# Last quarter of a feed-forward down product as five and two block products, with the second token half's norm and gate first

## The chip, the core and the metric

The kernel runs on one core of one Trainium2 chip. The metric is the device time of one launch in microseconds (us). The kernel before took 765.87 us (median of 3 runs, 765.47 to 766.1).

## The reference

One inference step of one encoder layer, for 512 prompt tokens and 64 sample tokens, 1024 features, float32. The part that matters here:

```python
x = layer_norm(ALPHA * x + mix @ w_o, ln1_g, ln1_b)
hid = square(relu(x @ w_up))                             # 1024 -> 4096
x = layer_norm(ALPHA * x + hid @ w_down, ln2_g, ln2_b)   # 4096 -> 1024
gate = sigmoid(x @ w_ple_gate + b_ple_gate)              # 1024 -> 1024
y = x + gate * (pe @ w_ple)
```

All 576 tokens go through it together; in the kernel features lie on the partitions and tokens along the free dimension. The attention ahead of it is the same in both kernels.

## The kernel before, in words

**Products.** Every operand is split into a high part (a cast to the rounded 32-bit matmul type) and a low part (the operand minus the high part), and each product is three matmuls per 128-row slice: high weight by high operand, high by low, low by high. `gemm` (L288) issues them and gives control back after every 6; that is one *tick*. `drive` counts ticks, runs the evacuations that were put off with `later(delay, ...)`, and lets a background generator (a layer norm) take steps in proportion.

**The feed-forward in quarters.** The 4096 hidden features come in eight groups of 512 (g = 0..7), two groups to a quarter (q = 0..3). For each quarter, `up_pair` makes the hidden features and `down_pair` adds their share of `w_down` to Y. From the second quarter on, and for the down products of the first three, a 2x2 block product (two 512-row halves of the contraction, two 128-column halves of the outputs, two 288-token halves A and B) is done by `seven` with seven block products in place of eight. A block product is 4 slices x 3 = 12 matmuls of 288 columns, two ticks; they come in the order 11, t0, t1, 21, t3, t2, 22. For them the operand has seven forms: three of its four quarters as they are and four sums (`operands`, L1339 to L1385: rows "11", "12", "22", "s1" to "s4"), each with a cast on ACT (L1351) and a subtraction on DVE (L1349), the sums on DVE too (L1364, L1372, L1374, L1379). The seven sums of the weights are made from three loads of 512, 512 and 256 KB, the first of them with a second, accumulating load on top (L210, from POOL's queue), and two DVE additions (L181, L184).

**The last quarter before.** Its hidden features are made by `seven` as well, but its down product is done plainly by `down_last`: the operand is only cast and subtracted (L1356, L1357), 8 weight units of 512 KB are loaded, and 192 matmuls follow for tokens 0 to 255 (A2), then 192 for tokens 256 to 575 (B2), each evacuated by L1631 on DVE.

**Norm and gate.** `LayerNorm` is a generator with hand-set waits: sums of Y over features (POOL at L1152 and L1154, the last sum and the fold at L1154 and L1159 on DVE), a mean by matmul (L1180), four subtractions (L1184), squares on ACT (L1186, L1189) and their sums (L1190), a variance by matmul (L1200), a square root and a reciprocal (L1202, L1203), a spread to all partitions by PE transposes (L56), and for each of four pairs of feature slices scale (DVE, L1216), gain and bias (ACT, L1227), cast (ACT, L1229) and subtraction (DVE, L1233). L2A (tokens A2) runs beside `down_last` of B2, L2B (tokens B2) beside the gate product of A2. `gate` and `gate_one` do 192 matmuls per token part, then a sigmoid (ACT, L1706, L1724), two DVE operations (L1709, L1710) and the store. PL, the per-layer embedding's product, is read back from DRAM (L1681, 2304 KB) after `seven`.

**What sets the order.** `Weights` is a planner: it loads weights ahead on SP's queue (L208) into four raw tiles of 512 KB (and one small one), and splits them piece by piece, one piece a tick, with a cast on ACT (L149) and a subtraction on DVE (L155; on POOL for units added with `pool_l`), into a ring of five tiles (`whl`). A unit may be split only when it is less than five units ahead of the oldest one in use, `lag` ticks after that one changed; an accumulated load counts as landed 13 ticks after its issue. Five more ring tiles (pool `fe`) come when the tiles of `seven` are given up. A scheduler then orders each engine's instructions, in which `high_priority` brings instructions forward; each engine runs its own list in order.

Of the kernel before, what the change touches and what calls it, by code (L numbers as in the profile page):

```python
# [14 lines left out]
D = 1024  # L15
# [21 lines left out]
def tile_hybrid_step(ctx: ExitStack, tc: tile.TileContext, I, O):  # L37
# [79 lines left out]
    class Weights:  # L117
# [74 lines left out]

        def load(self, issue=True, force=False):
# [176 lines left out]
    G_DOWN = 6  # L370
# [748 lines left out]
    A2, B2 = slice(0, 256), slice(256, NT)  # L1119
# [14 lines left out]
    class LayerNorm:  # L1134


        def __init__(self, sl, gi, waits):
# [3 lines left out]
            self.ready = -1  # L1141
            self.gen = self.steps()
            self.s = None

        def add(self, j):
# [3 lines left out]
            if j == 0:  # L1149
                self.s = lnp[0].tile([128, 2, 320], F32, name="ln_s", tag="ln_s" if self.sl.start else "relu", bufs=1 if self.sl.start else 2)[:, :, :self.w]  # L1150
            elif j == 2:
                (DVE if self.sl is A else POOL).tensor_tensor(self.s, y[:, 0:2], y[:, 2:4], OP.add)  # L1152
            else:
                (DVE if j == 6 or self.sl is A else POOL).tensor_tensor(self.s, self.s, y[:, j:j + 2], OP.add)  # L1154
# [17 lines left out]
        def steps(self):  # L1172
            sl, gi, w = self.sl, self.gi, self.w
            y = Y[:, :, sl]
# [8 lines left out]
            for j in range(0, 8, 2):  # L1183
                DVE.tensor_tensor(y[:, j:j + 2], y[:, j:j + 2], mb, OP.subtract)  # L1184
                if j == 0:
                    ACT.activation(ss, y[:, 0:2], AF.Square)  # L1186
                else:
                    sq = lnp[0].tile([128, 2, 320], F32, name="ln_sq", bufs=2)[:, :, :w]
                    ACT.activation(sq, y[:, j:j + 2], AF.Square)  # L1189
                    DVE.tensor_tensor(ss, ss, sq, OP.add)  # L1190
                if j == 6:
                    self.fold(ss)
# [18 lines left out]

            first = tc.high_priority if sl.start == 0 else ExitStack
# [95 lines left out]
    hid = {}  # L1308
# [5 lines left out]
    def sets(g):  # L1314

        if g >= G_DOWN:
            hid[g] = base.tile([128, 2, 4, NT], F32R, name="hidE", tag="AL") if g % 2 == 0 else \
                fb.tile([128, 2, 4, NT], F32R, name="hidO", tag="hidO")
            return
# [20 lines left out]
    def operands(g, m, t, v):  # L1340
# [12 lines left out]

        if g >= G_DOWN:
# [3 lines left out]
            return  # L1358
# [26 lines left out]
    def up_half(g, c, m, sl):  # L1385
        t = (A, B).index(sl)
        r = lnp[0].tile([128, 2, 320], F32, name="relu", bufs=2)[:, :, :HW]
# [149 lines left out]
    def up_pair(g, m):  # L1537
# [7 lines left out]
        def target(t):  # L1545
            return HX["f"][:, t, b] if g < G_DOWN and g % 2 == 0 else P.r[:, t]
# [62 lines left out]
    def down_last(sl, ln):  # L1609

        w = sl.stop - sl.start
        g0 = NG - 2
        ms = {}
        n = 0
        todo = [(j, 0) for j in (0, 2, 4)] + [(0, 1), (2, 1), (6, 0), (4, 1), (6, 1)]
        for j, part in todo:
            if part == 0:
                ms[j] = psum_g()
            m = ms[j]
            g = g0 + part  # L1620
# [212 lines left out]
```

## Time and profile before

| | us |
|---|---|
| median of 3 runs | 765.87 |
| the profiled execution's own time | 765.81 |
| its span | 764.1 |
| PE busy in the span | 751.4 |
| DVE busy | 571.4 |
| ACT busy | 472.6 |
| POOL busy | 110.6 |

The profile is one execution on the chip. PE's busy time includes the overlap of pipelined matmuls, so 98% busy does not say that PE runs at its peak; waits of PE are read from the list of waits and the chain. Durations of neighbouring DVE or ACT instructions overlap a little as well, so a merged row such as "3.02 x4" tells what four in a row cost. Line numbers (L288) are those of the kernel before. The span of 764.1 us and the 1.7 us around it make the execution's 765.81 us.

### The profile page before, as it was taken

How to read it: one execution, taken by the hardware profiler on the slowest of the kernel's cores; microseconds unless marked ns; L12 is line 12 of the kernel's file. 1: busy time of each engine (PE TensorE's matmuls, PEld its weight loads, DVE VectorE, ACT ScalarE, POOL GpSimd, SP SyncE). 2: the span in 40 equal slices, each digit the busy share in tenths (PEclk: the TensorE clock that was granted, in tenths of full speed). 3: DMA queues.
4: the chain of work that ended last, by engine and by line, in shares of the span. 5: the costliest groups of instructions: out<-in, count | busy, mean ns of one | idle time of the engine just before them, and what ended most of it. 6: DMA issues, size and time to landing. Idle time of an engine off the chain costs nothing.

```text
span 764.1 us, 14624 instructions
## 1 busy us (share of the span) xinstructions
PE 751.4 (98%) x5679; PEld 730.8 (96%) x5679; DVE 571.4 (75%) x1119; ACT 472.6 (62%) x931; POOL 110.6 (14%) x130
## 2 busy tenths in 40 slices
PE   9999999999999999999999999999999999999997
PEld 7999988999899999999999999999999999999997
DVE  6788888888777866779777579866898766657643
ACT  6589777897676535797654577435764466525451
POOL 7100324344241000100000000000000000011000
PEclk9999999999999999999999999999999999999999
DMA  8538354245222325352447666667667664731001
GB/s 284 171 69 152 125 141 121 91 138 173 88 86 81 110 64 174 116 171 86 111 111 178 148 158 175 147 161 184 157 143 181 152 151 152 286 113 30 28 29 69
DMA packets 38197, 101.35 MB, mean 133 GB/s; under 512 B 6000, under 2 KB 10224, under 8 KB 38000
## 3 DMA queue, kind: packets, MB, share of 16 engines
q1 hardware_dynamic: 34384, 87.61, 37.5%
q0 software_dynamic: 3456, 12.58, 10.2%
q8 instruction: 44, 0.72, 0.4%
q10 hardware_dynamic: 288, 0.22, 0.1%
q14 instruction: 25, 0.20, 0.1%
HBM read 85.26 MB, written 9.54 MB: 124 GB/s over the span
## 4 chain that ended last, share of the span: by engine, by line
PE 77%; DVE 13%; ACT 8%; issue 2%; DVEq 0%; ACTq 0%
PE g L288 40%; PE m L288 14%; PE n L288 13%; PE T L56 2%; DVE dbias L693 2%; ACT xr L771 2%; DVE whl L155 2%; DVE m L691 1%; PE V L958 1%; ACT whl L149 1%; PE m L452 1%; DVE sP L891 1%; PE m L466 1%; DVE x L774 1%; PE S L883 1%
## 5 line engine op out<-in xcount | busy, mean ns | idle before, releaser
L149 ACT CAST whl<-wraw 128x1024 fp32r<-128x1024 f32 (+2 forms) x190 | 154.9, 828 | 80.9 <-PE g L288 46.3
L155 DVE TENSOR_TENSOR whl<-wraw,whl 128x1024 fp32r<-128x1024 f32 (+2 forms) x158 | 157.7, 1008 | 53.3 <-ACT whl L149 52.6
L288 PE MATMUL m<-AH,whl 128*128 128x288 f32 x736 | 176.7, 307 | 0.0
L288 PE MATMUL g<-BH,whl 128*128 128x288 f32 (+2 forms) x768 | 160.0, 298 | 0.0
L288 PEld LDWEIGHTS m<-AH,whl 128*128 128x128 f32 x736 | 126.4, 188 | 1.7 <-issue 1.0
L288 PEld LDWEIGHTS g<-BH,whl 128*128 128x128 f32 x768 | 125.0, 188 | 1.5 <-ACT BH L1229 0.2
L288 PE MATMUL g<-BL,whl 128*128 128x288 f32 (+2 forms) x384 | 113.6, 296 | 0.6 <-DVE BL L1233 0.6
L288 PE MATMUL m<-AL,whl 128*128 128x288 f32 x368 | 108.8, 296 | 0.0
L288 PEld LDWEIGHTS g<-BL,whl 128*128 128x128 f32 x384 | 72.3, 188 | 1.2 <-DVE BL L1233 1.1
L288 PEld LDWEIGHTS m<-AL,whl 128*128 128x128 f32 x368 | 69.5, 189 | 0.7
L210 POOL DMA_DIRECT2D wraw<-in_w_dram x24 | 20.7, 864 | 287.5 <-DMA wraw<-in_w_dram 184.8
L896 ACT ACTIVATE sP<-sP,st 128x128 f32<-128x128 f32 (+4 forms) x72 | 39.4, 549 | 35.1 <-DVE st L891 35.0
L155 POOL TENSOR_TENSOR whl<-wraw,whl 128x512 fp32r<-128x512 f32 x32 | 42.2, 1333 | 89.2 <-ACT whl L149 85.0
L288 PE MATMUL m<-BH,whl 128*128 128x288 f32 x192 | 42.9, 302 | 0.0
L288 PE MATMUL g<-s,whl 128*128 128x288 f32 x288 | 42.1, 295 | 0.0
L288 PE MATMUL n<-BH,whl 128*128 128x288 f32 x192 | 42.0, 294 | 0.0
L288 PEld LDWEIGHTS g<-s,whl 128*128 128x128 f32 x288 | 39.5, 188 | 0.0
L56 PE MATMUL T<-ident,sP 128*128 128x128 f32 (+1 forms) x176 | 31.3, 274 | 1.5 <-DVE sP L905 0.6
L288 PEld LDWEIGHTS m<-BH,whl 128*128 128x128 f32 x192 | 32.0, 188 | 0.5 <-issue 0.3
L288 PEld LDWEIGHTS n<-BH,whl 128*128 128x128 f32 x192 | 32.0, 188 | 0.0
L1505 ACT ACTIVATE g<-n 128x288 f32<-128x288 f32 x24 | 9.5, 395 | 35.6 <-PE n L288 35.6
L288 PE MATMUL m<-BL,whl 128*128 128x288 f32 x96 | 28.3, 295 | 0.0
(327 smaller groups left out, 1624.1 us busy)
## 6 DMA issues: line engine op xcount, KB each, us to landing
wraw<-in_w_dram SPq DMA_DIRECT2D x48, 512.0 KB, 3.8
wraw<-in_w_dram POOLq DMA_DIRECT2D x24, 512.0 KB, 5.8
wraw<-in_w_qkv_dram SPq DMA_DIRECT2D x23, 512.0 KB, 3.6
wraw<-in_w_dram SPq DMA_DIRECT2D x24, 256.0 KB, 4.3
wraw<-in_w_up_dram SPq DMA_DIRECT2D x8, 512.0 KB, 4.1
wraw<-in_w_down_dram SPq DMA_DIRECT2D x8, 512.0 KB, 4.2
wraw<-in_w_gate_dram SPq DMA_DIRECT2D x8, 512.0 KB, 4.5
wraw<-in_w_o_dram SPq DMA_DIRECT2D x8, 384.0 KB, 3.0
```

Source lines behind the costliest of these rows:

```text
L56: PE.transpose(out, in_, ident[:n, :n])
L149: ACT.copy(self.hv[u][:, 0, c], src["tile"][:, c])
L155: eng.tensor_tensor(t[:, 1, c], src["tile"][:, c], f(t[:, 0, c]), OP.subtract)
L210: POOL.dma_start(t[:, :n], it["acc"], accum_op=OP.add)
L288: mm = PE.matmul(ps, W(w, kw, wc), a[:, ka, cols], start=(first and i == 0), stop=(last and i == n - 1), skip_group_check=more)
L452: PE.matmul(mk[:, h, :HW], w0(part, k), a[:, k, h * HW:(h + 1) * HW], start=(k == 0 and i == 0), stop=(k == 7 and i == 2))
L466: PE.matmul(acc[b][:n[b], :304], a[:, k, b * 128:b * 128 + n[b]], ixw(part, k), start=(k == 0 and i == 0), stop=(k == 7 and i == 2))
L691: tc.keep_in_program_order(DVE.max(m, s))
L693: tc.keep_in_program_order(DVE.match_replace(out=s, in_to_replace=m, in_values=s, imm_value=GONE))
L771: q(lambda r=r, s=s: ACT.mul(v2(xr[r * 32:r * 32 + 32]), v[s * 32:s * 32 + 32], sc))
L896: ACT.activation(j["P"], j["P"], AF.Exp, bias=j["st"][:, 0:1], scale=-1.0, accum_out=j["st"][:, 2:3])
L1505: ACT.mul(P.e, P.o, -1.0)
```

## The change

The last quarter's down product becomes 4 x 5 block products over all output pairs (`five`: 11, t0, t1, t3, t2) and then 4 x 2 (`two`: the rows "12" and "s4" with plain weight units of 256 output columns). The five finish the B half (tokens 288 to 575) of an output pair; the two complete the A half. The last two groups get the seven operand forms that the others have (L1356 and L1357 go), with the forms of `two` put off by 6 ticks. The weights for `five` are four units with one plain, one accumulated and one more plain load each (three of the four ring tiles that a unit of `seven` takes; one of them half filled and subtracted on POOL); those for `two` are four units of 512 KB subtracted on POOL, where there were eight subtracted on DVE. PL's load is issued before `five`. The norm of B (L2B, waits 5, 9, 3, its instructions at high priority, its work tiles carved out of two tiles of the feed-forward) runs beside `two`, the gate of B follows with the norm of A beside it, then the gate of A. Both token parts are 288 wide, where they were 256 and 320. The five extra ring tiles come after `two`, where they came ahead of `down_last`.

```diff
+        def add_five(self, ap):
+            u = len(self.cs)
+            self.cs += [128] * 3
+            r1 = self.source(ap[:, 0:1024], acc=ap[:, 1024:2048])
+            r2 = self.source(ap[:, 2048:3072])
...
+            self.split(u, r2, [lo], POOL)
+            self.split(u + 1, r1, [all2], DVE)
+            self.piece(u + 1, None, t1, r1, r2)
+            self.piece(u + 2, None, t2, r2)
+            self.split(u + 2, r2, [all2], DVE)
...
-        for kind, n in (("P", 4 if q else 0), ("Q", 4 if q < 3 else 0)):
+        for kind, n in (("P", 4 if q else 0), ("Q", 4)):
             for x in range(n):
-                U[kind, q, x] = WT.add_seven(I["w_7"][n7])
+                U[kind, q, x] = (WT.add_five if (kind, q) == ("Q", 3) else WT.add_seven)(I["w_7"][n7])
                 n7 += 1
-    for g in range(G_DOWN, NG):
-        for c in range(4):
-            U["D", g, c] = WT.add(I["w_down"][(g - G_DOWN) * 4 + c], 256, whole=True)
+    for c in range(4):
+        U["D", c] = WT.add(I["w_down"][c], 256, whole=True, pool_l=True)
...
-                (DVE if self.sl is A else POOL).tensor_tensor(self.s, y[:, 0:2], y[:, 2:4], OP.add)
+                self.eng.tensor_tensor(self.s, y[:, 0:2], y[:, 2:4], OP.add)
...
+                with (tc.high_priority if gi and self.soon else ExitStack)():
                     DVE.tensor_tensor(y[:, j:j + 2], y[:, j:j + 2], mb, OP.subtract)
...
-            first = tc.high_priority if sl.start == 0 else ExitStack
+            self.scaling = True
...
-        if g >= G_DOWN:
-            oh, ol = [hid[g][:, x, b, (A, B)[t]] for x in range(2)]
-            later(0, lambda: ACT.copy(oh, v))
-            later(0, lambda: DVE.tensor_tensor(ol, v, f(oh), OP.subtract))
-            return
...
-        split("12", v)
-        later(2, lambda: tt(v, v, F[0], OP.add))
+        d = 6 if g == NG - 1 else 0
+        split("12", v, d)
+        later(2 + d, lambda: tt(v, v, F[0], OP.add))
         if g > 1:
-            split("s4", v, 2)
+            split("s4", v, 2 + d)
...
+    def five(ln):
...
+        for c in range(4):
+            u = U["Q", 3, c]
+            y0, y1 = Y[:, 2 * c], Y[:, 2 * c + 1]
+            o = psum_n()[:, :HW]
+            yield from product(u, "11", o)
+            d = psM.tile([128, 2, 512], F32, name="g", tag="m", bufs=2)[:, 1, :HW]
+            with tc.high_priority():
+                ACT.copy(d, o)
+            oldest[0] = u + 1
+            later(0, lambda o=o, y0=y0: tt(y0[:, A], y0[:, A], o, OP.add))
+            z = psB.tile([128, 2, 512], F32, name="g", tag="g", bufs=1)[:, 0, :HW]
+            yield from product(u, "t0", z)
+            later(0, lambda z=z, y0=y0: tt(y0[:, B], y0[:, B], z, OP.add))
+            later(0, lambda z=z, y1=y1: tt(y1[:, B], y1[:, B], z, OP.subtract))
+            yield from product(u, "t1", d, False)
+            r = fs.tile([128, 2, 2, HW], F32, name="r", bufs=2)[:, 0, 0]
+            with tc.high_priority():
+                ACT.mul(r, d, -1.0)
+            e = psum_n()[:, :HW]
+            yield from product(u, "t3", e)
+            oldest[0] = u + 2
+
+            def both_halves(r=r, y1=y1):
+                y = y1.rearrange("p (a t) -> p a t", a=2)
+                tt(y, y, r[:, None, :].to_broadcast([128, 2, HW]), OP.add)
+            later(0, lambda r=r, e=e: tt(r, r, e, OP.add))
+            later(0, both_halves)
+            yield from product(u, "t2", d, False)
+            oldest[0] = u + 3
+
+            def last(d=d, y0=y0, c=c):
+                with tc.high_priority():
+                    tt(y0[:, B], y0[:, B], d, OP.add)
+                    ln.add(2 * c)
+            later(0, last)
+
+    def two():
+        for c in range(4):
+            W = unit_w(U["D", c])
+            m = psum_g()
+            for x, n in ((0, "12"), (1, "s4")):
+                for _ in gemm(m[:, x, :HW], W, range(4), HX[n][0], HX[n][1], slice(0, HW),
+                              wc=slice(x * 128, (x + 1) * 128)):
+                    WT.step()
                     yield 1
-            if part == 1:
-                def ev(j=j, m=m):
-                    y = Y[:, j:j + 2, sl]
-                    DVE.tensor_tensor(y, y, m[:, :, :w], OP.add)
-                    ln.add(j)
-                later(0, ev)
+            def ev(c=c, m=m):
+                y = Y[:, 2 * c:2 * c + 2, A]
+                DVE.tensor_tensor(y, y, m[:, :, :HW], OP.add)
+            later(0, ev)
...
     drive(seven(todo), len(todo) * 14, None, 0)
+    PL = base.tile([128, 8, NT], F32, name="PL", tag="AH")
+    SP.dma_start(PL.rearrange("p j t -> p (j t)"), PLD)
+    lnp[0] = Carved()
+    L2B = LayerNorm(B, 2, (5, 9, 3), True)
+    L2A = LayerNorm(A, 2, (5, 8, 2))
+    drive(five(L2B), 40, None, 0)
     WT.lag = 1
+    drive(two(), 16, iter(L2B), 32, False)
+    while not L2B.scaling:
+        L2B.pump()
     pS.close()
     fe = ctx.enter_context(tc.tile_pool(name="fe", bufs=1))
     WT.ring(fe, 0, 5, "e")
     lnp[0] = fe
-    PL = base.tile([128, 8, NT], F32, name="PL", tag="AH")
-    SP.dma_start(PL.rearrange("p j t -> p (j t)"), PLD)
-    L2A = LayerNorm(A2, 2, (4, 8, 2, 0))
-    L2B = LayerNorm(B2, 2, (5, 8, 2, 0))
-    drive(down_last(A2, L2A), 32, None, 0)
-    drive(down_last(B2, L2B), 32, iter(L2A), 28)
+    for j in (0, 2, 4, 6):
+        L2A.add(j)
...
-    drive(seq(gate(lo, A2, L2A), gate(hi, A2, L2A)), 32, iter(L2B), 25)
-    drive(seq(gate(lo, B2, L2B), gate((4, 5), B2, L2B), gate_one(6), gate_one(7)), 32, None, 0)
+    drive(seq(gate(lo, B, L2B), gate(hi, B, L2B)), 32, iter(L2A), 25)
+    drive(seq(gate(lo, A, L2A), gate((4, 5), A, L2A), gate_one(6), gate_one(7)), 32, None, 0)
```

More of the change, by code (lines that the diff above doesn't have):

```diff
@@ L1141, in __init__ @@
             self.ready = -1
+            self.soon, self.scaling = soon, False
+            self.eng = DVE if gi == 0 and sl is A else POOL
             self.gen = self.steps()
@@ L1173, in steps @@
             sl, gi, w = self.sl, self.gi, self.w
+            first = tc.high_priority if self.soon else ExitStack
             y = Y[:, :, sl]
@@ L1183, in steps @@
             for j in range(0, 8, 2):
[L1184 to L1192, printed above, removed]
+                with (tc.high_priority if gi and self.soon else ExitStack)():
+                    DVE.tensor_tensor(y[:, j:j + 2], y[:, j:j + 2], mb, OP.subtract)
+                    if j == 0:
+                        ACT.activation(ss, y[:, 0:2], AF.Square)
+                    else:
+                        sq = lnp[0].tile([128, 2, HW], F32, name="ln_sq", bufs=2)
+                        ACT.activation(sq, y[:, j:j + 2], AF.Square)
+                        DVE.tensor_tensor(ss, ss, sq, OP.add)
+                    if j == 6:
+                        self.fold(ss)
                 yield 1
@@ L1545, in target @@
         def target(t):
-            return HX["f"][:, t, b] if g < G_DOWN and g % 2 == 0 else P.r[:, t]
+            return HX["f"][:, t, b] if g % 2 == 0 else P.r[:, t]
         def t0():
@@ L1607, in down_pair, with __init__, tile @@
         return P
[L1609 to L1620, printed above, removed]
-            W = unit_w(U["D", g, j // 2], U["D", g0, 0] if sl is A2 else U["D", g0, j // 2])
-            for x in range(2):
-                for _ in gemm(m[:, x, :w], W, range(4), hid[g][:, 0], hid[g][:, 1], sl,
-                              wc=slice(x * 128, (x + 1) * 128), first=(part == 0), last=(part == 1)):
-                    n += 1
-                    WT.step(sl is B2 or n > 18)
-                    yield 1
-            if part == 1:
-                def ev(j=j, m=m):
-                    y = Y[:, j:j + 2, sl]
-                    DVE.tensor_tensor(y, y, m[:, :, :w], OP.add)
-                    ln.add(j)
-                later(0, ev)
+    class Carved:
+        def __init__(self):
+            a = fs.tile([128, 2, 4, HW], F32, name="lnA", tag="hF").rearrange("p a b c -> p (a b) c")
+            b = fs.tile([128, 2, 4, HW], F32, name="lnB", tag="s3").rearrange("p a b c -> p (a b) c")
+            self.parts = {"ln_s": [a[:, 0:2]], "ln_sq": [a[:, 2:4], a[:, 4:6]],
+                          "ln_r": [b[:, 0, 0:4], b[:, 0, 8:12]]}
+        def tile(self, shape, dt, name, tag=None, bufs=1):
+            p = self.parts[name]
+            p.append(p.pop(0))
+            return p[-1]
@@ new lines, in five, with product @@
+    def five(ln):
+        tt = DVE.tensor_tensor
+        oldest = [U["Q", 3, 0]]
+        def product(u, n, ps, first=True):
+            while owed.get(ROWS[n]):
+                pop_now()
+            x = HX[ROWS[n]]
+            W = WT.quarter(u, n, oldest[0])
+            for _ in gemm(ps, W, range(4), x[0], x[1], slice(0, HW), first=first, more=not first, pin=True):
+                WT.step()
+                yield 1
+        for c in range(4):
[31 more added lines that the diff above has]
+            later(0, last)
@@ L1763, in _laid_out @@
     out["w_up"] = units(w_up[:, :1024], 128)
-    out["w_down"] = np.concatenate([units(w_down[g * 512:g * 512 + 512], 256) for g in (6, 7)])
+    out["w_down"] = units(w_down[3584:], 256)
     def seven(w):
@@ L1774, in _laid_out @@
         s7 += [seven(w_up[:, n:n + 256]) for n in range(q * 1024, q * 1024 + 1024, 256) if q]
-        s7 += [seven(w_down[q * 1024:q * 1024 + 1024, n:n + 256]) for n in range(0, 1024, 256) if q < 3]
+        s7 += [seven(w_down[q * 1024:q * 1024 + 1024, n:n + 256]) for n in range(0, 1024, 256)]
     out["w_7"] = np.stack(s7)
```

46 lines of the change are left out of this document (23 added, 23 removed).

## The prediction

> **What bounds the kernel now.** I read the page first, then the list of PE's waits, then the work by stage, and only then single rows.
>
> ```profile
> span 764.1 us, 14624 instructions
> ...
> PE 77%; DVE 13%; ACT 8%; issue 2%; DVEq 0%; ACTq 0%
> ```
>
> The second line is the chain that ended last, by engine: three quarters of it is PE. What PE waited for after 300 us:
>
> ```profile
> PE n L288 <- DVE whl L155: 1.1, 2, 0.5
> PE n L288 <- DVE hC L1349: 0.8, 2, 0.4
> PE g L288 <- DVE BL L1233: 0.6, 2, 0.3
> ```
>
> The columns are us in total, times, longest. So 2.5 us of waits in 464 us: PE sets the time, and what it is given to do is what counts. The first two kinds come where the sevenfold down products begin, as here in the third of them (PE's timeline, the wait in brackets); the last comes where a norm hands over to its matmuls.
>
> ```profile
> 567.54 0.93 PE L288 MATMUL n<-hC,whl 128*128 128x288 f32 x5 [0.39 <-DVE hC L1349]
> ...
> 578.85 1.59 PE L288 MATMUL n<-hC,whl 128*128 128x288 f32 x10 [0.54 <-DVE whl L155]
> ```
>
> Now the stages:
>
> ```profile
> 562.70:573.90 11.20, 10.72 (x78) 10.27 (x78) 11.09 (x18) 7.17 (x12) 0.87 (x1) 1.00 0.69 165
> ...
> 654.15:676.99 22.84, 22.84 (x194) 22.84 (x193) 12.26 (x13) 9.49 (x11) 3.60 (x2) 1.00 0.77 281
> 676.99:706.25 29.26, 29.26 (x202) 29.20 (x201) 21.77 (x28) 14.03 (x22) 2.16 (x2) 1.00 0.12 37
> 706.25:730.86 24.61, 24.61 (x206) 24.45 (x205) 16.67 (x23) 12.38 (x19) 0.97 (x1) 1.00 0.07 23
> 730.86:759.72 28.86, 28.54 (x193) 28.01 (x192) 10.93 (x15) 9.31 (x19) 0.00 (x0) 1.00 0.17 59
> ```
>
> Columns: length, then busy us of PE, PEld, DVE, ACT and POOL, the granted clock, the DMA share and GB/s. The first row is the first output pair of the third sevenfold down product: DVE is busy 11.09 of 11.20 us, so PE is the bound there only just. The others are the plain product of A2 and of B2 and the gates of A2 and of B2: PE full, the other engines with room, and the rows of the waits say that PE lost 0.3 us in them.
>
> **The change: PE's work.** What a block product and the norm's own PE work cost:
>
> ```profile
> 644.62 1.59 PE g L288 x12
> ...
> 711.45 0.54 PE n L1180 x2
> ...
> 722.78 0.56 PE n L1200 x6
> ...
> 725.61 0.34 PE n L56 x3
> ```
>
> These are pieces of the chain that ended last. Twelve matmuls of 288 columns take 1.59 us. The plain product took 22.84 + 29.26 = 52.10 us (384 matmuls, and the mean, variance and transposes of L2A). In its place come 4 x 5 + 4 x 2 = 28 block products (336 matmuls), 28 x 1.59 = 44.5 us, and the norm's 0.54 + 0.56 + 0.34 = 1.4 us: 45.9 us. That is 6.2 us less. The gates keep their 384 matmuls; 192 of 256 columns and 192 of 320 become 384 of 288, the same number of columns. They took 24.61 + 28.86 = 53.47 us; 32 x 1.59 + 1.4 = 52.3 by the block product's row. I book half of the difference, 0.6 us: the 0.3 us of the wait on BL, which goes because the last gate's norm now has 32 ticks of 0.80 us beside it where it had 32 of 0.72 (23.2 / 32), and 0.3 for the shape. Together 6.8 us off PE's list.
>
> **The change: from the ups into the five.** Rows of the stage from 500 to 650 us, then POOL's subtraction (ns min/median/max):
>
> ```profile
> L155 DVE TENSOR_TENSOR whl<-wraw,whl 128x1024 fp32r<-128x1024 f32 x39 | 47.6, 1222 | 17.8 <-ACT whl L149 17.4
> L149 ACT CAST whl<-wraw 128x1024 fp32r<-128x1024 f32 x40 | 41.8, 1048 | 16.4 <-PE g L288 15.8 <-ACT whl L149 0.6
> ...
> L1585 DVE TENSOR_TENSOR Y<-Y,g 128x288 f32<-128x288 f32 x22 | 9.5, 449 | 8.7 <-PE g L288 8.7
> ...
> L155 DVE TENSOR_TENSOR whl<-wraw,whl 128x512 fp32r<-128x512 f32 x13 | 8.9, 683 | 0.0
> ...
> L1349 DVE TENSOR_TENSOR hC<-hF,hC 128x576 fp32r<-128x576 f32 x4 | 2.9, 755 | 0.1
> ```
> ```profile
> L155 POOL TENSOR_TENSOR whl<-wraw,whl x32: 1270/1286/1877, 77.8 to 226.0; 128x512 fp32r<-128x512 f32 x32
> ```
>
> The last two groups now make all seven forms, as groups 4 and 5 do, so the beginning of the five is read from the down product at 562.7 us: DVE has no room, and PE waits 0.4 us for a form and 0.5 us for the weights of the second pair's t1. In `seven` that t1 comes 9 products after the start, in `five` 7: 3.2 us sooner. Being 0.5 us late there, DVE must be rid of 3.7 us ahead of it. It is rid of one 1024-wide subtraction (1.22, now 512 wide on POOL), of two of 512 (2 x 0.68), 2.6 us in all, and of three operations on the forms put off by 6 ticks (3 x 0.755 = 2.3 us) if the scheduler lets those fall behind. So between 0 and 1.1 us late; 2.4 if POOL's 1.29 us is time in which DVE stands (see the rivals). With the 0.4 for the form, the loss is 0.4 to 2.8 us for this pair; the third pair inherits the forms that were put off (up to 1 us more), the fourth has no splits left on DVE. I take 1.8 us, nearer to the rows of 562.7 than to either end. ACT (1048 ns a cast, two and a half a pair in 8.0 us) is no bound.
>
> PL's load and the loads of the five share the DMA engines:
>
> ```profile
> PL<-PLD SPq DMA_DIRECT2D x1, 2304.0 KB, 9.3
> ```
>
> It lands 9.3 us after its issue, at the same point of SP's queue as before, behind the loads already issued. The five ask for 1.5 MB in 8.0 us where `seven` asks for 1.75 MB in 11.2: 0.69 x (188 / 156) = 0.83 of the DMA engines by the first row of the stages, plus PL in the first ten us. Raw tiles run two pairs ahead (16 us), so I cost this at nothing; if that cover is gone, the third pair waits for up to 3 us.
>
> **The change: L2B under the two.** This is the new place that decides. Rows of L2B before (640 = 2 x 320 columns; it will be 576, a factor of 0.9), on DVE and on ACT:
>
> ```profile
> 709.21 0.82 DVE L1154 TENSOR_TENSOR ln_s<-ln_s,Y 128x640 f32<-128x640 f32 x1
> 710.07 0.49 DVE L1159 TENSOR_TENSOR ln_s<-ln_s 128x320 f32<-128x320 f32 x1
> 712.03 3.02 DVE L1184 TENSOR_TENSOR Y<-Y,n 128x640 f32<-128x640 f32 x4 [1.47 <-PE n L1180]
> 714.96 2.68 DVE L1190 TENSOR_TENSOR ln_s<-ln_s,ln_sq 128x640 f32<-128x640 f32 x3
> 717.67 0.49 DVE L1159 TENSOR_TENSOR ln_s<-ln_s 128x320 f32<-128x320 f32 x1
> ...
> 725.98 3.02 DVE L1216 TENSOR_TENSOR Y<-Y,n 128x640 f32<-128x640 f32 x4 [2.12 <-PE n L56]
> 728.91 0.82 DVE L1233 TENSOR_TENSOR BL<-Y,BH 128x640 fp32r<-128x640 f32 x1
> ```
> ```profile
> 726.83 1.20 ACT L1227 ACTIVATE Y<-Y,gb 128x320 f32<-128x320 f32 x2 [3.19 <-DVE Y L1216]
> 728.07 0.73 ACT L1229 CAST BH<-Y 128x640 fp32r<-128x640 f32 x1
> ```
>
> Count from the end of the five. Last evacuation 0.45, last sum 0.74, fold 0.44, and 0.3 for the hand-overs: 1.9 us. The mean is placed behind 18 matmuls (2.4 us) and takes 0.5: 2.9. Subtractions, squares and sums ran 712.03 to 718.16, 6.13 us, now 5.5: 8.4. Variance to transposes, as close as their rows allow (0.56 and 0.34 on PE, two short ACT and DVE steps): about 1.6, so 10.0. First scale 0.7, gain and bias 1.08, cast 0.66, subtraction 0.74, hand-overs 0.3: the first pair is ready at about 13.5 us. The cover is 8 x 1.59 + 1.4 = 14.1 us. Alone, the chain just fits. But it is not alone: the first four gate units can be split only as the ring moves, that is inside the two (4 x 1.22 = 4.9 us of DVE, 4 x 1.05 of ACT), and four evacuations of 576 columns come as well (4 x 0.75 = 3.0). DVE's part of the chain is about 1.7 + 5.5 + 0.2 + 2.7 + 0.7 = 10.8; with the 7.9 that is 18.7 us of DVE in 14.1. About 3.4 of it (last evacuation, two scales, the fourth unit) can come later. So at least 1.2 us late; 3.8 if the subtraction of the last unit of the two, on POOL (two of 1.29), stands in DVE's way at the fold; up to 13.5 + 7.9 - 14.1 = 7.3 if everything is queued ahead of the chain, and 0 if the scheduler finds only gaps. I take 2.0, near the count.
>
> The norm of A has the gate of B beside it (16 x 1.59 = 25.4 us), and ACT and DVE had 12.4 and 16.7 us of work in 24.61; four weight units (4.2 and 4.9) and the rest of L2B move in, about 20 and 24 us. I cost that at nothing, 1 us if it fails. The tail behind the last matmul gets 10% shorter parts: under 0.1 us.
>
> **Sum.** 6.8 off, 1.8 and 2.0 back: 3.0 us. 765.81 - 3.0 = 762.8; the execution lies 0.06 under the median of 765.87, so 762.8 stands for the median as well.
>
> **Rivals.** *The covers hold*: both hand-overs cost 0.3 each, as the wait on BL did, and the time is 765.81 - 6.8 + 0.6 = 759.6. For it: ACT and POOL are little used, and the forms of the two are put off. Against it: the 11.09 of 11.20.
>
> *DVE and POOL stand in each other's way.* POOL, then DVE:
>
> ```profile
> 669.44 2.31 POOL L1152 TENSOR_TENSOR ln_s<-Y 128x512 f32<-128x512 f32 x1 [46.13 <-ACT whl L149]
> 675.14 1.29 POOL L1154 TENSOR_TENSOR ln_s<-ln_s,Y 128x512 f32<-128x512 f32 x1 [3.40 <-DVE Y L1631]
> 696.57 1.55 POOL L1152 TENSOR_TENSOR ln_s<-Y 128x640 f32<-128x640 f32 x1 [20.14 <-DVE Y L1631]
> ```
> ```profile
> 696.75 2.46 DVE L155 TENSOR_TENSOR whl<-wraw,whl 128x1024 fp32r<-128x1024 f32 x1 [0.26 <-ACT whl L149]
> ...
> 701.91 1.23 DVE L155 TENSOR_TENSOR whl<-wraw,whl 128x1024 fp32r<-128x1024 f32 x1 [0.31 <-ACT whl L149]
> ```
>
> The same DVE subtraction took 2.46 us when a POOL addition had begun 0.18 us before it, and 1.23 alone; POOL's addition took 2.31 beside one and 1.29 alone. They take turns, so POOL's new subtractions are no gift. A pair of the five then costs the two engines 2 x 1.22 + 2 x 0.69 (the two sums, as a 512-wide row) + 5 x 0.45 + 0.75 + 1.29 = 8.1 us against 8.0 of PE, with no room to make good the 2.8 us of the second pair: 2.8, and 0.9 each for the two after it, which also meet POOL's norm sums. 4.6 us in the five and 2.2 in the two give back all of the 6.8: 765.8. The Trainium skill, "GPSIMD Engine Reference", section "Key points", says that POOL shares its SBUF interfaces with VectorE and contends with those DVE instructions that read two SBUF inputs. By that rule only subtractions and sums are held up, not the evacuations from PSUM, and the price is lower than my 4.6; the two rows above are both of the kind it names, so the trace agrees as far as it goes.
>
> *L2B is not covered* (slower): the chain's links in the two lie behind all the splits and evacuations, at 7.3 us instead of 2.0, and PE stands in front of the gate of B: 765.81 - 6.8 + 1.8 + 7.3 = 768.1. It ends slower from a loss of 6.5 us there. For it: the 18.7 us in 14.1, ACT's four casts among the norm's 7 us of ACT work. Against it: high priority, and PE's own order, which need not wait at the variance while other matmuls are ready. The Trainium skill, "TensorE: Matmul & The Clock Gate", section "What's actually happening", says that PE's clock falls to half after an idle window of about 3.4 us and takes as long to rise; by that figure a standstill of that length would cost an estimated 1.7 us more. No run here shows it: the longest wait quoted above is 0.5 us, and the granted clock is 1.00 in every stage.
>
> **How the numbers follow.** Forecast 0.52 (761.3 to 764.3, from 1.5 us around the two taken losses), covers hold 0.13, in each other's way 0.20, not covered 0.15. About 0.2%, 1.5 us, is what a measurement can tell from no change. Faster: the first two, 0.65; same 0.20; slower 0.15. The range takes in most of the covers' case and reaches towards the slower one: 760.0 to 767.4, which leaves out some 0.1 on either side.
>
> **What would show it.** The stretch from the first block product of the five to the gate of B should be 45.9 us plus two visible losses: a wait of n or g on whl (L155) or a form in the second pair, and one on the norm (variance, BL of the first pairs, or whl of the third and fourth gate unit). Its DVE share should be near full at the start and in the two. The gates should take about 52.8 us. I am wrong if PE waits elsewhere for over 1 us (wraw loads, PSUM tiles, the gate of A), if the five run without a wait, or if the first gate matmul comes over 4 us after the last of the two.

## The result, and the profile after

The changed kernel took 777.02 us (median; 776.77 to 778.09). The kernel before took 766.13 us in the runs beside the first experiments (765.87 above). The ratio is 1.0144, with a 95% interval of [1.0131, 1.0156]: 11 us slower, where 3 us less were forecast. The profiled execution took 776.77 us (span 775.0 us), near the median. One execution of a later experiment (links first), 898.68 us at a mean granted clock of 0.75, is left out of the times below.

The chain that ended last, by engine: PE has 73% of it, where it had 77% before. The gemm line is now L308.

```profile
PE 73%; DVE 15%; ACT 7%; issue 3%; DMA 1%; DVEq 0%; ACTq 0%; POOLq 0%
```

What PE waited for after 300 us (us in total, times, longest):

```profile
PE g L308 <- ACT BH L1250: 3.7, 1, 3.7
PE n L1201 <- DVE lnA L1179: 3.4, 1, 3.4
PE g L308 <- ACT g L1656: 1.3, 1, 1.3
...
PE g L308 <- DVE hC L1365: 0.9, 1, 0.9
...
PE g L308 <- DVE whl L155: 0.9, 1, 0.9
...
PE g L308 <- ACT whl L149: 0.5, 1, 0.5
```

The list of before held 2.5 us, none longer than 0.5. This one has two waits of over 3 us, one ahead of L2B's mean and one ahead of the gate of B, and four of 0.5 to 1.3 in the five. The work by stage (five; two with L2B; gate of B; gate of A), columns as above:

```profile
654.77:691.90 37.13, 33.46 (x242) 32.09 (x241) 31.46 (x45) 18.36 (x27) 13.73 (x10) 1.00 0.65 199
691.90:715.21 23.31, 16.21 (x110) 15.64 (x108) 19.95 (x23) 10.43 (x15) 7.83 (x4) 0.93 0.42 136
715.21:741.20 25.99, 25.37 (x177) 25.03 (x178) 19.66 (x28) 15.16 (x24) 0.00 (x0) 0.93 0.12 44
741.20:770.40 29.20, 29.20 (x221) 28.87 (x219) 12.14 (x18) 11.91 (x23) 0.00 (x0) 1.00 0.16 56
```

Before, PE was full or nearly so in every stage at a granted clock of 1.00; now the first two stages have 3.7 and 7.1 us without PE, and two show a clock of 0.93. Close behind the two long waits the clock is lower still:

```profile
698.41:703.98 5.57, 5.57 (x29) 5.46 (x29) 4.78 (x8) 2.78 (x4) 0.00 (x0) 0.69 0.48 181
...
715.21:719.91 4.70, 4.08 (x18) 3.85 (x18) 4.70 (x8) 4.28 (x7) 0.00 (x0) 0.65 0.31 113
```

PE's timeline shows it in single rows: twelve matmuls behind the mean take 2.83 us, and 1.76 a few products later (rows of a timeline include the pipeline's overlap; 1.59 is the same block product on the chain).

```profile
698.41 0.75 PE L1201 MATMUL n<-lnA,onesm 128*128 128x288 f32 x2 [3.41 <-DVE lnA L1179]
699.27 2.83 PE L308 MATMUL g<-hB,whl 128*128 128x288 f32 x12
...
703.98 1.76 PE L308 MATMUL g<-hB,whl 128*128 128x288 f32 x12
```

Against the forecast's sum:

| stretch | forecast | after |
|---|---|---|
| start of the five (654.15 before) | 0 | +0.6 |
| five: 20 x 1.59, and 1.8 lost | 33.6 | 37.1 |
| two and norm: 8 x 1.59 + 1.4, and 2.0 lost | 16.1 | 23.3 |
| gates: 53.5 - 0.6 | 52.9 | 55.2 |
| behind the last matmul | 0 | +0.2 |

The differences, 0.6 + 3.5 + 7.2 + 2.3 + 0.2 = 13.8 us, on 762.8 make 776.6; the execution took 776.77. (The start of the five lay anywhere between 654.0 and 655.2 in the profiles that follow.)

Why the mean came late: DVE's timeline of after, then POOL's.

```profile
692.66 2.04 DVE L1174 TENSOR_TENSOR lnA<-lnA,Y 128x576 f32<-128x576 f32 x1
694.63 3.36 DVE L155 TENSOR_TENSOR whl<-wraw,whl 128x1024 fp32r<-128x1024 f32 x1
```
```profile
688.81 8.10 POOL L155 TENSOR_TENSOR whl<-wraw,whl 128x1024 fp32r<-128x1024 f32 x3
```

POOL subtracts three D units from 688.81 to 696.91. Beside it, DVE's last sum takes 2.04 us and the weight subtraction 3.36 (0.75 and 1.22 alone), both ahead of the fold. Why the gate came late: ACT's timeline just ahead of it.

```profile
711.55 1.04 ACT L149 CAST whl<-wraw 128x1024 fp32r<-128x1024 f32 x1 [1.89 <-PE g L308]
712.51 1.14 ACT L1248 ACTIVATE Y<-Y,gb 128x288 f32<-128x288 f32 x2
713.55 1.03 ACT L149 CAST whl<-wraw 128x1024 fp32r<-128x1024 f32 x1
714.49 0.67 ACT L1250 CAST BH<-Y 128x576 fp32r<-128x576 f32 x1
```

Casts of gate units that are needed later stand between L2B's links: 2.1 us, just before the cast for which PE waits.

### The profile page after: what moved, and what is told of

Its sections match the earlier page's. It is cut to its first block, busy times and chain, and to the rows that moved or that the text cites. A ratio compares the mean times of both kernels' runs of the same rounds, so it can differ in the third digit from the quotient of the medians.

```text
span 775.0 us, 14635 instructions
## 1 busy us (share of the span) xinstructions
PE 750.8 (97%) x5634; PEld 728.3 (94%) x5634; DVE 598.9 (77%) x1161; ACT 485.2 (63%) x953; POOL 129.3 (17%) x142
## 4 chain that ended last, share of the span: by engine, by line
PE 73%; DVE 15%; ACT 7%; issue 3%; DMA 1%; DVEq 0%; ACTq 0%; POOLq 0%
PE g L308 35%; PE m L308 14%; PE n L308 13%; DVE whl L155 3%; DVE dbias L711 2%; PE T L56 2%; ACT xr L789 2%; DVE m L709 1%; ACT whl L149 1%; PE V L976 1%; DMA wraw<-in_w_dram 1%; PE m L470 1%; PE m L484 1%; DVE sP L909 1%; DVE x L792 1%
## 5 line engine op out<-in xcount | busy, mean ns | idle before, releaser
L149 ACT CAST whl<-wraw 128x1024 fp32r<-128x1024 f32 (+2 forms) x198 | 161.3, 828 | 79.6 <-PE g L308 39.0
L155 DVE TENSOR_TENSOR whl<-wraw,whl 128x1024 fp32r<-128x1024 f32 (+2 forms) x158 | 161.5, 1031 | 43.1 <-ACT whl L149 42.5
L308 PE MATMUL m<-AH,whl 128*128 128x288 f32 x736 | 176.6, 307 | 0.0
L308 PE MATMUL g<-BH,whl 128*128 128x288 f32 x768 | 161.3, 299 | 3.7 <-ACT BH L1250 3.7
L308 PEld LDWEIGHTS g<-BH,whl 128*128 128x128 f32 x768 | 125.7, 189 | 5.5 <-ACT BH L1250 4.1
L308 PEld LDWEIGHTS m<-AH,whl 128*128 128x128 f32 x736 | 126.4, 188 | 1.7 <-issue 1.0
L308 PE MATMUL g<-BL,whl 128*128 128x288 f32 x384 | 114.2, 297 | 0.9 <-DVE BL L1254 0.9
L308 PE MATMUL m<-AL,whl 128*128 128x288 f32 x368 | 108.7, 296 | 0.0
L155 POOL TENSOR_TENSOR whl<-wraw,whl 128x512 fp32r<-128x512 f32 (+1 forms) x40 | 59.2, 1492 | 115.7 <-ACT whl L149 110.9
L230 POOL DMA_DIRECT2D wraw<-in_w_dram x28 | 24.3, 866 | 310.7 <-DMA wraw<-in_w_dram 223.2
L308 PEld LDWEIGHTS g<-BL,whl 128*128 128x128 f32 x384 | 72.8, 190 | 1.5 <-DVE BL L1254 1.3
L308 PEld LDWEIGHTS m<-AL,whl 128*128 128x128 f32 x368 | 69.5, 189 | 0.6
L308 PE MATMUL m<-BH,whl 128*128 128x288 f32 x192 | 43.0, 302 | 0.0
L308 PE MATMUL g<-s,whl 128*128 128x288 f32 x288 | 42.1, 295 | 0.0
L308 PE MATMUL n<-BH,whl 128*128 128x288 f32 x192 | 42.0, 294 | 0.0
L308 PEld LDWEIGHTS g<-s,whl 128*128 128x128 f32 x288 | 39.5, 188 | 0.0
L308 PE MATMUL g<-hB,whl 128*128 128x288 f32 x240 | 36.3, 301 | 0.0
L308 PEld LDWEIGHTS g<-hB,whl 128*128 128x128 f32 x240 | 34.0, 193 | 0.0
L308 PE MATMUL g<-hC,whl 128*128 128x288 f32 x192 | 29.2, 298 | 3.5 <-ACT g L1656 1.3
L308 PEld LDWEIGHTS m<-BH,whl 128*128 128x128 f32 x192 | 32.0, 188 | 0.5 <-issue 0.3
```

Of the source, the lines that this page charges most:

```text
L149: ACT.copy(self.hv[u][:, 0, c], src["tile"][:, c])
L155: eng.tensor_tensor(t[:, 1, c], src["tile"][:, c], f(t[:, 0, c]), OP.subtract)
L230: POOL.dma_start(t[:, :n], it["acc"], accum_op=OP.add)
L308: mm = PE.matmul(ps, W(w, kw, wc), a[:, ka, cols], start=(first and i == 0), stop=(last and i == n - 1), skip_group_check=more)
```

## The experiments

Theory A: POOL's subtractions stand in DVE's way (mean late). B: splits of gate units stand between L2B's links (gate late). C: each long wait is followed by a slow clock that costs PE time. D: an ACT cast that waits for a late load holds up what is queued behind it (wait on g in the third pair). The texts in front of each result say what was expected and what the rival would give.

**D units on DVE (A).**

```diff
-        U["D", c] = WT.add(I["w_down"][c], 256, whole=True, pool_l=True)
+        U["D", c] = WT.add(I["w_down"][c], 256, whole=True)
```

> The changed kernel with one thing undone: the four weight units of the two are subtracted on DVE, not on POOL. Theory 'POOL beside DVE': the mean of L2B waited 3.4 us because a sum (2.04 us) and a weight subtraction (3.36 us) on DVE stood beside POOL's subtractions; without them the wait at the mean is under 1 us, the clock stays at 1.00 behind it, and the time falls by 4 to 5.5 us, to about 772. Rival 'too much work for DVE in the two, on whichever engine': the wait only moves on to the variance or the gate, and the time falls by less than 2 us.

772.22 us, ratio 1.0078 [1.0063, 1.0093]: 4.8 us less. Its DVE timeline has the sum at 0.75 and the subtraction at 1.22, and the wait ahead of the mean is gone from its list:

```profile
PE g L308 <- ACT BH L1250: 4.7, 1, 4.7
PE g L308 <- ACT g L1656: 2.5, 1, 2.5
```

A is shown, although DVE got more to do: the stage of the two fell from 23.3 to 19.5 us (692.07 to 711.53). The wait ahead of the gate grew by 1.0 and that of the third pair by 1.2. The edit does not touch the third pair; its wait hangs on a load (theory D), and was 0.6 us in the next two experiments, which do not touch it either. So 1 us or more between two kernels can be this load alone.

**No splits of gate units (B).** The gates multiply by the last unit of the two; the loads and splits of the gate units are left out, so y is not the reference's.

```diff
-        U["G", c] = WT.add(I["w_gate"][c], 128, whole=True)
...
-        Ws = {c: unit_w(U["G", c], U["G", 0] if sl is B else U["G", cs[0]]) for c in cs}
+        Ws = {c: Unit(WT.hv[U["D", 3]], 128) for c in cs}
```

> The changed kernel without the loads and splits of the eight gate units; both gates multiply by the last unit of the two instead, so y is not the reference's. Theory 'the gate units' splits lie ahead of L2B's links': both waits (mean 3.4, first BH of the gate 3.7 and BL 0.6) fall below 1 us each, with them the slow clock, and the time falls by 8 to 11 us, to 766 to 769. Rival 'the chain itself is longer than the two': the wait ahead of the gate of B stays over 2 us.

772.58 us, 1.0082 [1.0067, 1.0097]: 4.4 us less, where 8 to 11 were expected. Its PE waits:

```profile
PE n L1199 <- DVE lnA L1177: 3.6, 1, 3.6
PE g L308 <- DVE BL L1252: 1.1, 1, 1.1
...
PE g L308 <- ACT BH L1248: 0.6, 1, 0.6
```

The gate's wait falls from 3.7 to 0.6 with 1.1 behind it, and the mean's stays. So A and B are separate causes. Of the 4.4 us, 1.0 lies in the five (36.15 us for 37.13, the shorter wait for the load in the third pair) and is not B's. The mean's wait stayed because the fold itself now stands beside POOL:

```profile
691.80 2.40 DVE L1172 TENSOR_TENSOR lnA<-lnA,Y 128x576 f32<-128x576 f32 x1
694.23 2.48 DVE L1177 TENSOR_TENSOR lnA<-lnA 128x288 f32<-128x288 f32 x1
```

**Useless matmuls in the two waits (C).** 24 ahead of the mean and 26 ahead of the gate of B, on data that is there.

```diff
+    def idle_matmuls(n):
+        t = psum_n()
+        for _ in range(n):
+            tc.keep_in_program_order(PE.matmul(t[:, :HW], BH[:, 0, 0:128], BH[:, 0, A], start=True, stop=True))
```

> The changed kernel with 24 matmuls of no use ahead of the mean of L2B and 26 ahead of the gate of B, where PE stood still for 3.4 and 3.7 us. Theory 'the standstill lowers the clock': the granted clock, 0.69 and 0.65 in the stretches behind the two waits, stays at 1.00, and the time falls by the 1.7 + 1.7 us that the slow matmuls cost, to about 773.5, although nothing waits for less long. Rival 'the slow stretches have another cause' (what runs there beside PE): the stretches stay slow and the time is within 1 us of 777.0.

775.50 us, 1.0125 [1.0108, 1.0142]: 1.5 us less. The rows behind mean and gate, to be held against the 0.69 and 0.65:

```profile
698.00:702.00 4.00, 3.83 (x27) 3.73 (x28) 3.16 (x6) 2.21 (x4) 0.00 (x0) 1.00 0.64 247
...
715.00:719.00 4.00, 3.87 (x27) 3.64 (x28) 4.00 (x6) 3.97 (x7) 0.00 (x0) 1.00 0.02 4
```

That the standstill brings the slow clock is shown. By stages of the profiled runs the gates took 53.2 us (714.95 to 768.14) for 55.2, the two 24.1 for 23.3, and the five 36.0 for 37.1; the last is again the load in the third pair (its wait 0.6 for 1.3) and not the useless matmuls. Only one of the two slow stretches was worth time: with full clock behind the mean the gate of B still began at 714.95 (715.21 in after). L2B's links on DVE and ACT, not PE, set its start, as PE's wait of 1.2 us on BH behind the useless matmuls shows.

**The copy ahead of the cast (D).** The cast of the fourth pair's accumulated weights is issued behind the third pair's copy.

```diff
-                    ACT.copy(self.hv[u][:, 0, c], src["tile"][:, c])
+                    with tc.issue_after(self.behind[u]) if u in self.behind else ExitStack():
+                        ACT.copy(self.hv[u][:, 0, c], src["tile"][:, c])
...
-                ACT.copy(d, o)
+                cp = ACT.copy(d, o)
+            if c == 2:
+                WT.behind[u + 4] = cp.ins
```

> The changed kernel with one order on ACT: the cast of the fourth pair's accumulated weights is issued behind the copy of the third pair's first product, not ahead of it, where it waited for its load until 677.6 us. Theory 'a cast that waits for its load holds up the copy': the wait of 1.3 us at the third pair's t1 goes and the time falls by 1 to 1.5 us. Rival 'the late load is the bound': the same wait comes back in the fourth pair, as a wait on whl, and the time is the same within 0.5 us.

775.50 us, 1.0122 [1.0107, 1.0137]: 1.5 us less, and the wait of 1.3 us is gone. ACT's timeline of after shows what it had been, a cast that waited 3.04 us for its load with the copy behind it:

```profile
677.64 1.04 ACT L149 CAST whl<-wraw 128x1024 fp32r<-128x1024 f32 x1 [3.04 <-DMA wraw<-in_w_dram]
678.59 0.39 ACT L1656 COPY g<-n 128x288 f32<-128x288 f32 x1
```

**Hold: A and D mended, late gate units held back.** The two edits above; besides, the casts of gate units 4 to 7 are issued behind the first BH cast of L2B, their subtractions behind the first BL.

```diff
+                if self.soon and gi and j == 0:
+                    for c in range(4, 8):
+                        WT.low_behind[U["G", c]] = last.ins
...
+            if self.soon and gi:
+                for c in range(4, 8):
+                    WT.behind[U["G", c]] = chain[0]
```

> The two edits before together (units of the two subtracted on DVE, the third pair's copy ahead of the cast) and a third: the splits of the last four gate units, which are needed only half a gate later, are issued behind the first cast (ACT) and the first subtraction (DVE) of L2B. Theory 'late gate units stand ahead of L2B's links on ACT and DVE': the first link of the gate of B comes 3 us sooner, its wait falls from 4.7 to 2 us or less, the clock stays high, and the time is 772.2 - 1.4 - 4.5, about 766.3. Rival 'the first four gate units and the evacuations are what fills the two': the wait stays over 3.5 us, the time at 770 or more.

769.99 us, 1.0049 [1.0034, 1.0064]; 766.3 was expected. The gate's wait fell only from 4.7 to 3.1, and the copy's wait went, but one of 0.9 on the negation (r) came, because the cast now stands ahead of that:

```profile
PE g L311 <- ACT BH L1253: 3.1, 1, 3.1
...
PE g L311 <- ACT r L1677: 0.9, 1, 0.9
```

The rest stands in its DVE timeline: subtractions of units 1 and 2 between the last sums of squares put the second fold at 703.70, and that of unit 3 comes just ahead of the scales (L1240).

```profile
699.42 1.22 DVE L158 TENSOR_TENSOR whl<-wraw,whl 128x1024 fp32r<-128x1024 f32 x1
700.56 0.75 DVE L1215 TENSOR_TENSOR lnA<-lnA 128x576 f32<-128x576 f32 x1
...
702.56 1.22 DVE L158 TENSOR_TENSOR whl<-wraw,whl 128x1024 fp32r<-128x1024 f32 x1
703.70 0.45 DVE L1182 TENSOR_TENSOR lnA<-lnA 128x288 f32<-128x288 f32 x1
...
705.55 1.20 DVE L158 TENSOR_TENSOR whl<-wraw,whl 128x1024 fp32r<-128x1024 f32 x1
706.66 2.74 DVE L1240 TENSOR_TENSOR Y<-Y,n 128x576 f32<-128x576 f32 x4
```

**The start of the five.** Three kernels on top of the hold: the 512-wide subtraction of the five on DVE; the forms of the last two groups put off by 16 ticks instead of 6; both.

```diff
-            self.split(u, r2, [lo], POOL)
+            self.split(u, r2, [lo], DVE)
...
-        d = 6 if g == NG - 1 else 0
+        d = 16 if g == NG - 1 else 0
```

> The kernel of the hold with the 512-wide subtractions of the five on DVE too, so that POOL splits nothing. Theory 'POOL and DVE take turns': a subtraction on POOL (1.3 to 2.0 us) costs DVE more than its own 0.68, the waits of the second pair (0.9 + 0.5 on the weights) shrink and the time falls by 0.5 to 1.5 us. Rival 'POOL's subtraction is hidden': DVE, busy without a gap there, gets 0.6 us more a pair and the time rises by 0.5 to 1.5 us.

> The kernel of the hold with the forms of the two put off by 16 ticks in place of 6. Theory 'DVE is the bound at the beginning of the five': three operations of 0.75 us leave the queue ahead of the second pair's weights, the waits there (0.9 on a form, 0.9 and 0.5 on weights) fall by 1 to 2 us, and so does the time. Rival 'the accumulated load is the bound there': the waits stay and the time is the same within 0.5 us.

> The kernel of the hold with both edits, no split on POOL and the forms of the two put off by 16 ticks. If both theories hold, the gains add up: 1.5 to 3 us less than the hold alone, about 764. If the loads are the bound, or POOL's work is hidden, it is within 1 us of the hold.

773.65 us (1.0094 [1.0079, 1.0109]), 769.61 (1.0046 [1.0031, 1.0060]) and 773.57 (1.0092 [1.0076, 1.0109]). Putting the forms off changed nothing: the same form operations came at the same places of DVE's list, so it tells nothing of DVE. What it does show is that the scheduler does not let these forms fall behind. With the subtraction on DVE, the wait on the form hC fell from 0.9 to 0.3 us and the one on whl from 0.9 to 0.5, as A would have it, but a new one of 3.2 us came (4.0 with both edits), which neither theory had: ACT's list now had a cast that waits 2.53 us for a load ahead of the cast that the second pair needs. It is D again, at another place, and behind it the clock was 0.50 from 670 to 676 us.

**Links first, PL late, and the causes taken out.** On top of the hold: subtractions of gate units 1 and 2 behind the second fold and of unit 3 behind the first BL, and the cast of D behind the third pair's negation instead of its copy; then PL's load written behind the five as well. The third kernel is the changed one with the D units on DVE, without gate units (as above), and with the cast behind the negation.

```diff
+                            for c in (1, 2):
+                                WT.low_behind[U["G", c]] = fold
...
-                    for c in range(4, 8):
+                    for c in range(3, 8):
...
-    lnp[0] = Carved()
...
+    PL = base.tile([128, 8, NT], F32, name="PL", tag="AH")
+    SP.dma_start(PL.rearrange("p j t -> p (j t)"), PLD)
     drive(two(), 16, iter(L2B), 32, False)
```

> The kernel of the held splits (769.99 us) with two more orders set: the subtractions of gate units 1 and 2 come behind the norm's second fold and that of unit 3 behind the first BL, and the fourth pair's accumulated cast comes behind the third pair's negation on ACT instead of behind its copy. Theory that DVE's order inside the two products sets the gate's start: the fold comes at about 701.3 instead of 703.7, the gate of B 2.3 us sooner (wait on BH under 1 us), and the wait on the negation (0.9 us) goes: 766.8 us. Rival, that ACT's chain of squares, casts and gain sets it: the wait on BH stays at 2.5 us or more, and only the 0.9 us go: 769.1 us.

> The same with the 2304 KB load of PL issued behind the five instead of ahead of them. Theory that PL's load delays the third pair's accumulated weights and with them ACT's queue: the third pair's accumulating load starts some 4 us sooner, the waits of the second and third pair on whl (0.5 and 0.9 us) shrink by 0.5 to 1.4 us in all: 765.8 us. Rival, that the late weights come from DVE's being full (raw tiles given back late) or that the cover holds as forecast: no difference over 0.3 us.

> The changed kernel with all three named causes out at once: the D units' subtractions on DVE, no loads and splits of the gate units (the gates multiply by the last unit of the two, so y is not the reference's), and the fourth pair's accumulated cast behind the third pair's negation on ACT. If the three causes are all there is, and the forecast's count of PE's work (45.9 us for five, two and norm) is right: 766.1 - 6.8 + 2.3 (the waits left in the five: form 0.9, whl 0.9 and 0.5) + 0.6 (later start of the five) + 0.5 (hand-over to the gate) = 762.7 us, 761.7 to 763.7. Rival, that the causes only hide others (DVE's total, 18.7 less 4.9 in 14.1, still too much): a wait of 2 us or more stays ahead of the gate of B, 764.7 us or more.

Links first: 769.18 us (768.1 to 770.8), ratio 1.0042 [1.0027, 1.0058], its profiled run 768.28; 766.8 was expected. PL late: 768.56 us, 1.0038 [1.0025, 1.0052]. Causes out: 768.46 us, 1.0030 [1.0017, 1.0044].

With the links first, the fold came at 701.21 and the wait on BH fell from 3.1 to 1.4 us, so DVE's order did set the gate's start, although the time lies at the rival's 769.1. The other edit did not do what it says: the cast is put on ACT's list before the negation exists, so nothing was held and the wait on the copy came back (1.4 us). With PL late it was 0.7, the only wait that changed; the times of the two kernels can't be told apart. But this edit did not do what it says either. The statement moved, the load did not: the scheduler issued it at the same time, in links first and in PL late alike (SP's timeline of each).

```profile
650.83 0.33 SPq L1756 DMA_DIRECT2D PL<-PLD  x1
651.20 0.33 SPq L1761 DMA_DIRECT2D PL<-PLD  x1
```

So the theory about PL's load is untested, and the 1.4 and 0.7 are one order of work, up to that wait, measured twice. The causes-out kernel missed its 762.7 by far, with 1.7 us of that copy among its waits (the same edit), 0.6 and 1.1 at the gate, and 2.3 in the five.

Its gates, and those of the links-first kernel, show what was new. In links first, behind waits of 1.42 us on BH and 0.41 on BL, the clock fell to half:

```profile
706.96:709.00 2.04, 1.63 (x7) 1.42 (x8) 2.04 (x4) 2.04 (x4) 0.62 (x2) 0.77 0.34 135
709.00:711.00 2.00, 2.00 (x10) 2.00 (x9) 2.00 (x2) 2.00 (x4) 1.78 (x1) 0.50 0.18 31
711.00:713.00 2.00, 2.00 (x15) 2.00 (x15) 2.00 (x3) 2.00 (x5) 0.00 (x0) 0.88 0.63 231
```

**Mended.** PL written late (its load began at 650.98, as ever), the cast of D behind the copy again, and 10 useless matmuls ahead of the gate of B.

```diff
+            if c == 2:
+                WT.behind[u + 4] = cp.ins
...
+        if sl is B and cs[0] == 0:
+            idle_matmuls(10)
```

> The kernel with the links first and PL late (768.56 us; profiled run 768.15), with the fourth pair's accumulated cast behind the third pair's copy (its wait there was 0.7 us) and 10 useless matmuls ahead of the gate of B, to fill the wait of 1.4 us. Theory that a wait of 1.4 us with another of 0.4 close behind it already lowers the clock (0.50 for some 3.4 us in the gate's first matmuls) and that this slow stretch lies on the path: 1.6 us come back, and up to 0.7 from the copy: 766.3 us, no difference from the kernel before that can be told. Rival, that the slow stretch costs nothing because ACT and DVE pace the gate's first matmuls anyhow: only the 0.7 comes back, 767.9 us.

767.76 us, 1.0023 [1.0014, 1.0032] beside 765.78 for the kernel before: at the rival's 767.9, still slower than before. The profiled run took 768.32, the slowest of eleven. Its stages (two stretches at the second pair of the five; the two; the gates):

```profile
669.00:671.00 2.00, 1.89 (x10) 1.89 (x11) 1.13 (x2) 0.89 (x1) 0.23 (x1) 0.72 0.59 174
671.00:674.80 3.80, 3.80 (x23) 3.80 (x22) 3.00 (x7) 1.91 (x3) 0.65 (x1) 0.70 0.90 182
...
691.40:707.39 15.99, 15.89 (x119) 15.45 (x118) 15.43 (x23) 8.84 (x13) 1.27 (x1) 1.00 0.47 143
707.39:761.98 54.59, 53.58 (x395) 52.48 (x395) 34.07 (x47) 28.51 (x48) 2.44 (x2) 1.00 0.16 57
```

The clock at the gate is whole, and the third pair waits for nothing. But the second pair's two waits, 0.75 and 0.87 us here, now bring a slow clock in the five (0.72 and 0.70 for 5.8 us), though not in every execution: the mean clock was 0.997 here and 1.000 in four of the eleven. In this run it takes back what the copy gave, so the rival's number is met partly by chance. The gates give back only 0.4 us (54.6 for 55.0), since waits on BL and on the sum of L2A, 1.0 us in all, stand in them.

## Why the prediction was wrong

**Right.** PE's work: with the mends the two and the norm take 15.99 us, 14.1 of work and 1.9 lost (1.3 of it filled with the useless matmuls), where 16.1 were forecast. That the 1.9 is so near the 2.0 booked is luck: it took three changes of order to get there. The two places where the change would pay, a second pair of the five and L2B, are where it paid. DVE and POOL do take turns.

**The step that failed first** is "L2B under the two", 2.0 us. It measured 9.2 (23.3 - 14.1), beyond its bound of 7.3. The count of "18.7 us of DVE in 14.1" was sound as a count; what failed was taking the loss "near the count", as if work that can come later would be placed later. ACT and DVE run their lists in order, and splits that no one needed yet stood ahead of the links. The stage of the two shows what each was worth: 23.3 us as changed, 19.5 with the D units on DVE, 17.8 with the late gate units held back (the whole time fell by 2.2 us, 769.99 for 772.22, but that has D's mend in it), and 16.0 with the links first. The rival "DVE and POOL stand in each other's way" had the other half right and priced it too low, at 2.2 us in the two: 4.8 by the D units alone, because the fold, on which all of L2B hangs, was behind one sum and one subtraction stretched from 2.0 to 5.4 us in all. The Trainium skill, "GPSIMD Engine Reference", section "Key points", limits the contention to DVE instructions in a two-port mode or with two SBUF inputs. The trace agrees: the stretched rows read two tiles of SBUF, or two parts of one, and this evacuation from PSUM, beside the same POOL row, is not stretched. (One row with two inputs from SBUF, the sum into Y at 691.06, kept its 0.76 us; it began 0.15 us before POOL ended the first of the three subtractions, at 688.81 + 2.40.)

```profile
692.11 0.45 DVE L1681 TENSOR_TENSOR Y<-Y,g 128x288 f32<-128x288 f32 x1 [0.28 <-PE g L308]
```

**The clock.** The rival "L2B is not covered" (slower) was the nearest, and named the mechanism that the forecast held to be absent: "No run here shows it". Now runs do. With the useless matmuls the gates took 2.0 us less, 0.6 of it the wait on BL, which went too; the 1.4 left for the slow stretch are near the 1.7 estimated. The section "What's actually happening" of "TensorE: Matmul & The Clock Gate" in the Trainium skill has the clock fall after an idle window of about 3.4 us. Halving and a slow stretch of some 3.5 us agree with the rows (once it was over 6 us); the length of the idle time does not: 1.42 + 0.41 us with 0.4 us of matmuls between them did it, and 0.75 + 0.87 with 0.5 between, while a single wait of 1.66 us in the third pair of the causes-out kernel left 1.00. Nor does the sum of the idle time alone decide: waits of 0.62 and 1.06 us at the gate of the causes-out kernel brought 0.50, and 0.62 and 1.07 at the gate of the kernel without gate units left 1.00. The same page of the Trainium skill says that the window runs freely. Its phase would explain such a pair, but was not tried.

**"From the ups into the five"**, 1.8 us, measured 5.3 (37.1 - 31.8). The form cost 0.9 instead of 0.4 and the second pair's t1 0.5 and 0.9. Each costs more than its listed wait, as PE's timeline of after shows:

```profile
657.95 1.35 PE L308 MATMUL g<-hC,whl 128*128 128x288 f32 x7
660.20 0.93 PE L308 MATMUL g<-hC,whl 128*128 128x288 f32 x5 [0.90 <-DVE hC L1365]
```

Seven matmuls of 0.133 us (1.59 / 12) would be through at 658.88; the next begins at 660.20, 1.32 us later, and the list says 0.90. Counted in this way the first two pairs lose 3.5 us, beyond the bound of 2.8, and the third 1.4. The third pair's is the "cost at nothing, up to 3 us if that cover is gone": ACT was held to be "no bound" by its sum of work, and a queue in order made it one, by one cast waiting for a late load. How much of that wait is due to PL's load is open, as no run moved it. The second pair's loss is left in all kernels. DVE's timeline of after shows two steps that failed there, beside POOL's row:

```profile
663.26 0.76 DVE L1365 TENSOR_TENSOR hD<-r,hD 128x576 fp32r<-128x576 f32 x1
663.93 2.32 DVE L155 TENSOR_TENSOR whl<-wraw,whl 128x1024 fp32r<-128x1024 f32 x1
...
666.54 0.68 DVE L205 TENSOR_TENSOR wraw<-wraw 128x512 f32<-128x512 f32 x1
```
```profile
663.86 1.31 POOL L155 TENSOR_TENSOR whl<-wraw,whl 128x512 fp32r<-128x512 f32 x1 [0.48 <-ACT whl L149]
```

The form hD, which only the two need, was to "fall behind"; it stands ahead of the sum (L205) for which the second pair's cast waits. And POOL's 512-wide subtraction costs DVE 1.1 us (2.32 for 1.22), and 1.0 once before (653.97, 2.23), which the forecast had only in its upper bound. Where this subtraction went from POOL to DVE the sum began 10.4 us after the start of the five instead of 11.8, and the waits of DVE fell, but ACT's order spoilt the gain. How the 3.5 us divide among DVE's own work, the forms and POOL's turns stays open.

**The gates** were booked 0.6 us cheaper; as changed they took 2.3 us more than forecast, from the slow clock and the wait on BL. With full clock they take 54.6 in the mended kernel, of which 1.0 is waiting, and 53.2 with the useless matmuls of C, where the list has no wait in them: 0.3 less than before (53.5), half of the 0.6.

The whole loss in short: 7.2 more in the two than forecast, 3.5 in the five, 2.3 in the gates, and 0.8 at the ends. Mended, the first is gone (15.99 for 16.1), and the other two leave the kernel 0.2% behind the one before.

## What to carry to other kernels

When a change shortens PE's work, the cover of everything beside it shrinks by as much; here 6.2 us less on PE laid 18.7 us of DVE into 14.1. Don't price such a place by the sum of the work: write down the list of each engine in order, and ask for each link of the critical chain what stands ahead of it and whether that can itself be waiting for a load. Two waits close together that add up to 1.6 us or more, or one of over 3 us, are to be priced with a fall of the clock behind them. And look into the trace whether an edit moved what it names: three of the edits here (the forms put off, the cast behind the negation, PL late) moved nothing.

## What the runs showed of the hardware

- PE's granted clock fell to 0.50 behind pairs of waits that added up to only 1.6 to 1.8 us, and rose again after some 3.5 us; but one such pair (0.62 + 1.07) and a single wait of 1.66 us left it at 1.00. Ten matmuls in the gap kept it at 1.00.
- Beside POOL's 1024-wide subtractions (8.10 / 3 = 2.7 us each) DVE's operations with two inputs in SBUF took 2.04 to 3.36 us instead of 0.75 to 1.22, and a fold of 288 columns 2.48 instead of 0.45: 1.3 to 2.1 us more in the rows shown, whatever their size. Beside the 512-wide ones (1.3 us) it was 1.0 to 1.1 more.
- By the starts of the matmuls PE lost 0.2 to 0.6 us more around a wait than the 0.5 to 1.3 us that the list gives for it.
- The wait in the third pair, which hangs on one load, was 0.6 to 2.5 us in kernels whose order of work up to it is the same.
